# Holding back the modulation-weight loads while value tiles are turned through a DRAM scratch, in a one-core decoder layer

## The chip, the cores and the metric

The kernel runs on one core of a Trainium2 chip. The metric is the device time of one execution in microseconds. The kernel before was timed in three runs: 1776.6, 1780.31 and 1783.93 us, median 1780.31 us.

## What is computed

The reference is one layer of a decoder trunk, in float32, applied to a prompt of 256 tokens and to 8 single decode tokens (264 columns in all), with a model width of 2048. Cut to what matters here:

```
mod = silu(c) @ w_ada + b_ada                       # w_ada: 2048 x 12288, six 2048-wide rows of results
sh1, sc1, gt1, sh2, sc2, gt2 = split(mod, 6)
h = rmsnorm(x, g_pre_mix) * (1 + sc1) + sh1
z = h @ w_in                                        # inputs, gates and values of three token mixers
y_a = u * (W_s @ layernorm(v) + b)                  # mixer A: spatial gating
y_b = head_norm(gated recurrence, 8 heads) * silu   # mixer B (HGRN2)
y_c = head_norm(gated recurrence, 4 heads) * silu   # mixer C (GLA)
merged = sum_n sigmoid(z_gate[n]) * (y_n @ w_branch[n])
x  = x + gt1 * rmsnorm(merged @ w_out, g_post_mix)
h2 = rmsnorm(x, g_pre_mlp) * (1 + sc2) + sh2
x  = x + gt2 * rmsnorm(relu(h2 @ w_mlp_up)**2 @ w_mlp_down, g_post_mlp)
```

The six rows of `mod` are called rows 0 to 5. Rows 0 and 1 are needed at once; row 2 (gt1), 3 (sh2) and 4 (sc2) when the mixer half ends; row 5 (gt2) at the very end. The states of the recurrences are outputs too.

## The kernel before

**The stream.** Every large product takes its weights, 512 KB at a time, from `Stream` (L641): a load on SyncE's queue (L671) into one of four `raw` buffers, a rounded copy by ScalarE (`whi`, L679) and the rest by VectorE (`wlo`, L683), and then 24 matmuls into a PSUM tile `mm` (`granule`, L719). Such a step of 512 KB is called a granule. The counter `now` (L433) counts granules: `linear` (L813) runs granules one by one and calls `background()` (L791) after each, which adds one to `now` and does the side work that is due.

**The side work.** `background()` pumps three queues of generators: `bg` (the mixers' vector work), `bs` (the decode tokens' states) and `bt` (turning of tiles and tails). It calls `slot()` (L753) where small products have gathered: those of the mixers' levels, those of the decode states, and the modulation products. It ends with `rounds.tick()`.

**The modulation rounds.** `Rounds` (L371) computes rows 2, 3 and 4 of `mod` beside the mixers, 16 steps for each row. A step is 1 MB of `w_ada` in two loads of 512 KB on SyncE's queue (`load`, L379, the DMA on L388) and 16 recorded matmuls into `ada` (`steps`, L408). Steps are gathered into batches. The first of a batch goes into one of the two `araw` buffers, the others into blocks `b` of the general pool of 28 blocks. `tick` (L404) loads the next step when the batch is not full and `gap` (or `pace`) granules have gone by since the last load, `due` (L399) says that a full batch may be multiplied `land` granules after its last load. In the mixers `gap` is 2 and the batch is 1 where levels or decode states were pending in the last six granules, else 2; after branch 1, `pace` and the batch are 4. What is left when the output projection ends is loaded and multiplied at once by `rounds.drain()` (L1749). Row 5 has rounds of its own, six steps of which are loaded during the output projection (L1741).

**The value tiles.** Matmuls need some tiles with tokens on the partitions. `Rows` (L843) turns a block of 512 KB: VectorE transposes 32x32 squares (L856), `out` (L858) writes the block to the scratch `rows_d` in DRAM by one DMA of GpSimd's queue (L859), and `back` (L861) reads it with the squares in their new places by four DMAs of 128 KB on the same queue (L865). `come` (L881) waits at least `TURN_OUT` = 2 granules between the two, and whoever uses the tile waits `TURN_IN` = 2 granules after `back`. Eleven blocks are turned so while modulation rounds run: the values of both HGRN2 groups and of GLA, the decayed keys `kd` of each group, and the mixers' outputs.

**Order.** In the mixer and branch part (from L1182 to L1627) the order of instructions is written by hand on TensorE and GpSimd alone; on SyncE, ScalarE and VectorE the scheduler that builds the program places them, so a load can be issued ahead of one that was written before it. The same holds, with TensorE alone by hand, for the output projection (L1729 to L1754).

Of the kernel before, what the change touches and what calls it, by code (L numbers as in the profile page):

```python
# [57 lines left out]
LEVELS_HELD = 3  # L58
FETCHED = 3
AGE = 2  # L60
ADA_LAND = 4
FETCH = 256
FETCH_AT = 105
# [9 lines left out]
def hybrid_step_kernel(  # L73
# [11 lines left out]
    class Products:  # L85
# [4 lines left out]
        def matmul(self, out, w, x, **kw):  # L90
            self.n += 4 if w.dtype == F32 else 2
            return nc.tensor.matmul(out, w, x, **kw)  # L92
# [32 lines left out]
    def blk(shape=None, dt=F32):  # L125
        shape = shape or [P, 4, NT]
        return blkp.tile(shape, dt, tag="b", name=nm("b"))
# [118 lines left out]
    def rstd_small(ms, scale, out):  # L246

        n, w = out.shape
        xx, aa = tmp([P, 16], "sx")[0:n, 0:w], tmp([P, 16], "sa")[0:n, 0:w]
        c = 0  # L250
        for m in ms if isinstance(ms, list) else [ms]:
            V.tensor_scalar(xx[:, c:c + m.shape[1]], m, scale, EPS, ALU.mult, ALU.add)
            c += m.shape[1]
        V.tensor_scalar(out.bitcast(I32), xx.bitcast(I32), -0.5, 1597463007.0, ALU.mult, ALU.add)
        for _ in range(3):
            mul(aa, out, out)
            V.scalar_tensor_tensor(aa, aa, -0.5, xx, ALU.mult, ALU.mult)
            V.scalar_tensor_tensor(out, aa, 1.5, out, ALU.add, ALU.mult)
# [112 lines left out]
    class Rounds:  # L371
# [3 lines left out]
        def __init__(self):  # L375
            self.todo, self.ws, self.done, self.at = [], [], None, 0
            self.pace, self.batch, self.gap, self.land = 5, 1, 0, ADA_LAND

# [20 lines left out]
        def due(self):  # L399
            if self.ws:  # L400
                return self.full() and now[0] >= self.at + self.land
            return self.done is not None and not self.todo and now[0] >= self.at + 2 * ADA_LAND

        def tick(self):  # L404
            if self.todo and not self.full() and now[0] >= self.at + (self.gap or self.pace):
                self.load()

        def steps(self, n=None):  # L408
# [21 lines left out]

    rounds = Rounds()

    now = [0]  # L433

    class Queue:

# [316 lines left out]
    def slot():  # L753

        lv = [x for x in levels if x[0] + AGE <= now[0]][:2]
        sv = [x for x in samples if x[0] + AGE <= now[0]]
        late = max([now[0] - x[0] for x in lv] + [0]) >= AGE + SLOT_WAIT + 3
        while lv and not T.room(LEVEL_N * len(lv) + 16 * len(sv)) and (len(lv) == 2 or not late):
# [32 lines left out]
    def background():  # L791
# [10 lines left out]
        bs.pump(rate[1])  # L802
        wait = max([now[0] + 1 - AGE - x[0] for x in levels + samples] + [0])
        if not levels and samples and rounds.ws and rounds.full() and not rounds.due():
# [38 lines left out]
    class Rows:  # L843
# [13 lines left out]

        def out(self, i):  # L858
            nc.gpsimd.dma_start(rows_d[self.d0 + i], self.ts.pop(i))  # L859

        def back(self, i):  # L861

            t = blk([P, 1024])
            for q in range(4):
                nc.gpsimd.dma_start(  # L865
                    t[32 * q:32 * q + 32, :].rearrange("p (s c) -> p s c", s=4),
                    rows_d[self.d0 + i].rearrange("(s p) (q c) -> q p s c", s=4, q=4)[q],
                )
            self.rows.append(t.rearrange("p (s r k f) -> p r k s f", s=4, r=2, k=4))
            self.at = now[0]  # L870

        def gone(self):

            for i in range(len(self.blks)):
                for r in range(2):
                    self.half(i, r)
                    yield
                self.out(i)
            self.at = now[0]
# [676 lines left out]
    def branch(n, parts):  # L1556
        for m in range(8):
            if m == 0:
                yh, yl = parts()
            z = zin(9232 + n * D + m * CW)  # L1560
            gt = tmp([P, 2, NT], "gt")
            S.activation(gt, z, AF.Tanh, scale=0.5)
            pr = linear(w_branch[0, n], 0, 8, m * CW, CW, yh, yl)
            if n == 0 and m % 2 == 0:
                mg[m // 2] = blk()
            dst = pair(mg[m // 2], m % 2)

            if n == 0:
                V.scalar_tensor_tensor(dst, gt, 1.0, pr, ALU.add, ALU.mult)
            else:  # L1570
                V.scalar_tensor_tensor(gt, gt, 1.0, pr, ALU.add, ALU.mult)
                add(dst, dst, gt)
            if n == 2 and m % 2 == 1:
                a, b = blk(dt=F32R), blk(dt=F32R)
                split_tokens(mg[m // 2], a, b)
                mh.append(a)
                ml.append(b)
# [15 lines left out]
    def parts_b(gates):  # L1593
        for i in range(2):
            finish(i)
            o = Gs[i].o[0]
            V.scalar_tensor_tensor(o, o, hgnT, gates[i], ALU.mult, ALU.mult)
        return yparts([Gs[0].o[0], Gs[1].o[0]])
# [19 lines left out]
    narrow[1] = False  # L1618
    rounds.land = ADA_LAND + 1
    branch(1, lambda: parts_b(gates_b))  # L1620
# [461 lines left out]
```

## Time and profile before

| What | Value |
|---|---|
| median of three runs | 1780.31 us |
| the profiled execution | 1781.23 us |
| its span, first to last instruction | 1779.4 us |
| TensorE busy with matmuls | 1754.1 us (99%) |
| VectorE, ScalarE, GpSimd busy | 1197.1, 996.9, 184.7 us |
| mean granted TensorE clock | 0.998 |
| moved by DMA | 458.89 MB, mean 258 GB/s |
| loads of modulation weights by `Rounds` | 128, of 512 KB each |
| writes to the scratch, reads from it | 16 of 512 KB, 64 of 128 KB |

The span is what the profile's rows add up over; 1.8 us of the execution lie outside it. A row such as "PE mm L92" is a group of matmuls that go through the helper on line 92 and write a tile named `mm`; `ada` are the modulation products and `sm` the small products. SPq and POOLq are the instructions by which SyncE and GpSimd start a DMA. `x24` is a count. A number in brackets behind a row of the timeline is the time for which the engine had nothing to run before it, and behind the arrow stands what ended that.

### The profile page before, as it was taken

The page shows a single profiled execution, that of the slowest core. Times are in us where ns is not written, and L with a number is a line of the kernel's source. Part 1 is how long each engine was busy: PE and PEld are TensorE (multiplying, and loading weights), DVE is VectorE, ACT ScalarE, POOL GpSimd, SP SyncE. Part 2 cuts the span into 40 slices and gives each one's busy share as a digit, 9 for nine tenths or more (in the row PEclk, how much of TensorE's full clock was granted, in tenths as well). Part 3 has the DMA queues.
Part 4 walks back from the last instruction along what each step waited for, and adds up shares of the span by engine and source line. Part 5 has one row for each costly group of instructions (what it writes and reads, how often), then busy time and mean ns, then how long its engine had stood idle before and what let it go on. Part 6 is the DMA issues. An engine that isn't in the chain of part 4 may idle for free.

```text
span 1779.4 us, 43024 instructions
## 1 busy us (share of the span) xinstructions
PE 1754.1 (99%) x17334; PEld 1690.4 (95%) x17334; DVE 1197.1 (67%) x2105; ACT 996.9 (56%) x1808; POOL 184.7 (10%) x308
## 2 busy tenths in 40 slices
PE   7999999999999999999999999999999999999998
PEld 5899999999999999999999989999999999999997
DVE  5676779886787785566556666545666666666666
ACT  5444466776776666555445666545454545454544
POOL 4222011122121112210000010000000000000001
PEclk9999999999999999999999999999999999999999
DMA  9998877899998899998886847776666666666665
GB/s 349 400 349 296 281 245 237 285 314 315 317 305 266 301 326 304 332 356 275 281 281 215 310 125 235 238 260 201 192 200 192 199 192 198 194 197 195 196 196 167
DMA packets 335560, 458.89 MB, mean 258 GB/s; under 512 B 16226, under 2 KB 278224, under 8 KB 335360
## 3 DMA queue, kind: packets, MB, share of 16 engines
q1 hardware_dynamic: 312160, 381.05, 65.4%
q0 software_dynamic: 22560, 74.63, 12.2%
q8 instruction: 136, 2.23, 0.5%
q14 instruction: 64, 0.52, 0.1%
q10 hardware_dynamic: 640, 0.47, 0.1%
HBM read 435.99 MB, written 20.09 MB: 256 GB/s over the span
## 4 chain that ended last, share of the span: by engine, by line
PE 91%; DMA 4%; issue 3%; DVE 2%; ACT 1%; POOL 0%; SPq 0%; DVEq 0%; POOLq 0%; ACTq 0%
PE mm L92 82%; PE ada L92 5%; PE sm L92 4%; DMA raw<-in_w_in_dram 2%; DMA b<-in_w_ada_dram 1%; DMA rows_d<-b 1%; DVE wlo L683 1%; PE sm L96 1%; DMA b<-in_x_prompt_dram 0%; DVE b L142 0%; DMA b<-in_gla_w_up_dram 0%; DVE b L1821 0%; POOL b L865 0%; ACT whi L679 0%; DVE b L1358 0%
## 5 line engine op out<-in xcount | busy, mean ns | idle before, releaser
L92 PE MATMUL mm<-b,whi 128*128 128x264 f32 x9248 | 1577.9, 277 | 6.2 <-ACT whi L679 2.2
L92 PEld LDWEIGHTS mm<-b,whi 128*128 128x128 f32 x9248 | 1395.5, 189 | 26.3 <-issue 12.4
L92 PE MATMUL mm<-b,wlo 128*128 128x264 f32 x4624 | 1276.5, 276 | 0.2 <-DVE wlo L683 0.2
L683 DVE TENSOR_TENSOR wlo<-raw,whi 128x512 fp32r<-128x512 f32 x1118 | 756.6, 688 | 427.3 <-ACT whi L679 420.6
L679 ACT CAST whi<-raw 128x512 fp32r<-128x512 f32 x1118 | 679.6, 617 | 624.8 <-DVE wlo L683 312.1
L92 PEld LDWEIGHTS mm<-b,wlo 128*128 128x128 f32 x4624 | 874.2, 189 | 0.7 <-DVE wlo L683 0.4
L142 DVE TENSOR_TENSOR b<-b,mm 128x528 f32<-128x528 f32 (+1 forms) x137 | 95.4, 697 | 57.9 <-PE mm L92 51.7
L859 POOL DMA_DIRECT2D rows_d<-b x16 | 9.1, 566 | 776.8 <-DVE b L1698 685.3
L92 PE MATMUL ada<-b,cT 128*32 128x256 f32 (+1 forms) x1152 | 66.3, 367 | 2.4 <-DMA b<-in_w_ada_dram 2.1
L92 PEld LDWEIGHTS ada<-b,cT 128*32 128x32 f32 x1152 | 35.4, 112 | 25.1 <-DMA b<-in_w_ada_dram 5.6
L540 POOL DMA_DIRECT2D b<-in_w_ada_dram x64 | 46.3, 727 | 43.2 <-PE ada L92 32.6
L1319 POOL DMA_DIRECT2D out_dram<-st x32 | 23.5, 735 | 205.9 <-DVE st L1318 187.0
L865 POOL DMA_DIRECT2D b<-rows_d x64 | 35.2, 556 | 46.4 <-DMA rows_d<-b 20.5
L679 ACT CAST whi<-araw 128x512 fp32r<-128x512 f32 x38 | 23.2, 619 | 27.3 <-PE mm L92 23.4
L1318 DVE SCALAR_TENSOR_TENSOR st<-vbc,b,st 128x128 f32<-128x128 f32 (+1 forms) x96 | 32.3, 389 | 6.3 <-DMA vbc<-vs_d 4.4
L139 DVE TENSOR_TENSOR b<-b,b 128x512 f32<-128x512 f32 (+1 forms) x49 | 34.4, 717 | 2.3 <-ACT b L1385 1.0
L1316 ACT ACTIVATE st<-st,fs 128x128 f32<-128x128 f32 (+1 forms) x96 | 35.2, 426 | 0.0
L92 PE MATMUL ada<-araw,cT 128*32 128x256 f32 x512 | 34.8, 382 | 0.0
L683 DVE TENSOR_TENSOR wlo<-araw,whi 128x512 fp32r<-128x512 f32 x38 | 24.5, 685 | 1.3 <-ACT whi L679 1.3
L145 DVE TENSOR_TENSOR b<-b 128x1024 f32<-128x1024 f32 (+1 forms) x24 | 24.4, 1018 | 0.6 <-PE ada L92 0.4
L145 DVE TENSOR_TENSOR b<-gt,b 128x528 fp32r<-128x528 f32 x32 | 22.7, 708 | 3.1
L1895 ACT ACTIVATE b<-vt 128x528 fp32r<-128x528 f32 x32 | 22.8, 712 | 1.0
(312 smaller groups left out, 823.0 us busy)
## 6 DMA issues: line engine op xcount, KB each, us to landing
raw<-in_w_in_dram SPq DMA_DIRECT2D x225, 512.0 KB, 5.7
raw<-in_w_mlp_down_dram SPq DMA_DIRECT2D x128, 512.0 KB, 3.5
raw<-in_w_mlp_up_dram SPq DMA_DIRECT2D x125, 512.0 KB, 3.7
araw<-in_w_ada_dram SPq DMA_DIRECT2D x64, 512.0 KB, 6.8
b<-in_w_ada_dram SPq DMA_DIRECT2D x64, 512.0 KB, 7.0
b<-in_w_ada_dram POOLq DMA_DIRECT2D x48, 512.0 KB, 9.8
raw<-in_w_branch_dram SPq DMA_DIRECT2D x48, 512.0 KB, 5.5
raw<-in_w_out_dram SPq DMA_DIRECT2D x32, 512.0 KB, 4.9
```

The costliest lines, as they stand in the source:

```text
L92: return nc.tensor.matmul(out, w, x, **kw)
L139: V.tensor_tensor(o, a, b, op=ALU.mult)
L142: V.tensor_tensor(o, a, b, op=ALU.add)
L145: V.tensor_tensor(o, a, b, op=ALU.subtract)
L540: queue.dma_start(w[:, i], w1[k * P:(k + 1) * P, :, self.k0 * P:(self.k0 + self.n) * P])
L679: self.last = [S.copy(hi, raw).ins, None]
L683: self.last[1] = V.tensor_tensor(lo, raw, hi.bitcast(F32), op=ALU.subtract).ins
L865: nc.gpsimd.dma_start(t[32 * q:32 * q + 32, :].rearrange("p (s c) -> p s c", s=4), rows_d[self.d0 + i].rearrange("(s p) (q c) -> q p s c", ...
L1316: S.activation(st[:, i, :], st[:, i, :], AF.Copy, scale=fs[:, h0 + i, b:b + 1])
L1318: V.scalar_tensor_tensor(st[:, i, :], v[:, i, :], k[:, h0 + i, NP + b:NP + b + 1], st[:, i, :], ALU.mult, ALU.add)
L1319: nc.gpsimd.dma_start(G.s_out(b, h0, nh), st)
L1895: S.activation(apart(a), by_two(rl), AF.Square)
```

## The change

A second counter, `passes`, holds the granule up to which modulation weights are not asked for. Writing a block out sets it to three granules from now, reading one back sets it to two from now, and `tick` loads nothing before that granule. Nothing else is changed: `due`, `steps`, `drain` and `load` stay, and the loads of row 5 that are made by `pre.load` do not go through `tick`.

```
+PASS_OUT, PASS_IN = 3, 2
...
         def tick(self):
-            if self.todo and not self.full() and now[0] >= self.at + (self.gap or self.pace):
+            if self.todo and not self.full() and now[0] >= max(self.at + (self.gap or self.pace), passes[0]):
                 self.load()
...
-    now = [0]
+    now, passes = [0], [0]
...
         def out(self, i):
             nc.gpsimd.dma_start(rows_d[self.d0 + i], self.ts.pop(i))
+            passes[0] = now[0] + PASS_OUT
...
         def back(self, i):
...
             self.rows.append(t.rearrange("p (s r k f) -> p r k s f", s=4, r=2, k=4))
             self.at = now[0]
+            passes[0] = now[0] + PASS_IN
```

More of the change, by code (lines that the diff above doesn't have):

```diff
@@ L60 @@
 AGE = 2
+PASS_OUT, PASS_IN = 3, 2
 ADA_LAND = 4
@@ L404, in tick @@
         def tick(self):
-            if self.todo and not self.full() and now[0] >= self.at + (self.gap or self.pace):
+            if self.todo and not self.full() and now[0] >= max(self.at + (self.gap or self.pace), passes[0]):
                 self.load()
@@ L431, in hybrid_step_kernel @@
     rounds = Rounds()
-    now = [0]
+    now, passes = [0], [0]
     class Queue:
@@ L859, in out @@
             nc.gpsimd.dma_start(rows_d[self.d0 + i], self.ts.pop(i))
+            passes[0] = now[0] + PASS_OUT
         def back(self, i):
@@ L870, in back @@
             self.at = now[0]
+            passes[0] = now[0] + PASS_IN
         def gone(self):
```

## The prediction

> **What bounds the kernel now.** I read the page first, then TensorE's waits while the modulation rounds run (280 to 930 us), then the chain and the two queues around the one large wait.
>
> ```profile
> PE 1754.1 (99%) x17334; PEld 1690.4 (95%) x17334; DVE 1197.1 (67%) x2105; ACT 996.9 (56%) x1808; POOL 184.7 (10%) x308
> ```
>
> TensorE is busy for 1754.1 of a span of 1779.4 us, and the change removes no matmul. It can only gain where TensorE stands still, or runs slowly, because a load came late. Between 280 and 930 us TensorE's waits are these:
>
> ```profile
> PE mm L92 <- ACT whi L679: 2.2, 1, 2.2
> PE mm L92 <- ACT gt L1562: 0.9, 1, 0.9
> PE mm L92 <- ACT b L1253: 0.8, 1, 0.8
> PE mm L92 <- DVE wlo L683: 0.2, 1, 0.2
> ```
>
> Four waits, 4.1 us in all: that is nearly the whole prize. The wait for `L1253`, 0.8, is for ScalarE's eviction and not for a load; I leave it. The other three I follow to their place. In the timeline of TensorE they are:
>
> ```profile
> 598.22 0.49 PE L92 MATMUL mm<-b,whi 128*128 128x264 f32 x2 [2.20 <-ACT whi L679]
> 598.94 0.38 PE L92 MATMUL mm<-b,wlo 128*128 128x264 f32 x1 [0.23 <-DVE wlo L683]
> ...
> 766.67 0.49 PE L92 MATMUL mm<-b,whi 128*128 128x264 f32 x2 [0.90 <-ACT gt L1562]
> ```
>
> The first two are one stall. The windows and the chain show what follows it (the column after the four engines' and GpSimd's busy times is the granted clock, then the DMA engines' share and GB/s):
>
> ```profile
> 596.00:598.00 2.00, 0.01 (x1) 0.00 (x0) 0.00 (x0) 0.45 (x1) 0.00 (x0) 1.00 1.04 372
> 598.00:600.00 2.00, 1.55 (x8) 1.35 (x9) 1.80 (x3) 2.00 (x6) 0.00 (x0) 0.85 0.79 279
> 600.00:602.00 2.00, 2.00 (x11) 2.00 (x11) 2.00 (x5) 0.88 (x2) 0.00 (x0) 0.50 0.20 47
> ```
> ```profile
> 581.25 16.20 DMA raw<-in_w_in_dram
> ...
> 598.94 4.41 PE mm L92 x22
> ...
> 605.58 10.80 PE mm L92 x96
> ...
> 617.08 2.90 PE mm L92 x24
> ```
>
> At full clock 96 matmuls take 10.80 us, so a granule of 24 takes 2.70 and 22 take 2.48; behind the stall 22 took 4.41, at a granted clock of 0.50. So the stall costs 2.20 + 0.23 + 1.93 = 4.36 us. It ends when a stream load lands that was 16.20 us under way, where the usual is 5.7:
>
> ```profile
> raw<-in_w_in_dram SPq DMA_DIRECT2D x225, 512.0 KB, 5.7
> ...
> araw<-in_w_ada_dram SPq DMA_DIRECT2D x64, 512.0 KB, 6.8
> ```
>
> What lay before that load, on SyncE's queue and on GpSimd's, and how full the DMA engines were:
>
> ```profile
> 574.56 0.94 SPq L388 DMA_DIRECT2D araw<-in_w_ada_dram  x2
> 576.39 1.58 SPq L671 DMA_DIRECT2D raw<-in_w_in_dram  x2
> 578.01 2.45 SPq L388 DMA_DIRECT2D b<-in_w_ada_dram  x2
> 581.25 19.77 SPq L671 DMA_DIRECT2D raw<-in_w_in_dram  x5
> ```
> ```profile
> 575.49 0.56 POOL L859 DMA_DIRECT2D rows_d<-b  x1 [17.75 <-DVE b L856]
> ...
> 584.53 2.19 POOL L865 DMA_DIRECT2D b<-rows_d  x4 [4.69 <-DMA rows_d<-b]
> ```
> ```profile
> 580.00:585.00 5.00, 5.00 (x47) 5.00 (x46) 1.96 (x3) 4.87 (x6) 0.47 (x1) 1.00 1.03 379
> ```
>
> Two modulation steps (four loads, 2 MB) were asked for within 5 us, in the very granules in which a tile went out at 575.49 and came back at 584.53, and the DMA engines were full (share 1.03, 379 GB/s). This is the collision that the change is about.
>
> **The change part by part.** I count granules through the code. The tile that goes out at 575.49 does so in granule 110 and comes back in 113; the four loads above are asked for in 109 and 111. An earlier tile goes out in 102 and comes back in 105. Around here the modulation loads now come every four granules (a batch of one, `land` 4), then two granules apart in a batch of two.
>
> *The hold itself.* The first load that is held is that of granule 41; it goes in 42. Out in 60, 62, 66 and 70 and back in 65, 68, 69 and 75 then shut the loads off nearly without a break: what was loaded in 61, 66 and 68 now goes at about 73 and 77. That makes the rounds 8 granules late. Out 102 and back 105 hold the next load to 107; out 110 and back 113 hold the one after it to 115. So in 108 to 114 no step is asked for, where there were two, and the whole 2 MB (5.5 us at 379 GB/s) is gone from in front of the load of 581.25. Landing at 597.45 becomes about 592; the copy and the rest take 0.62 and 0.69 us,
>
> ```profile
> L683 DVE TENSOR_TENSOR wlo<-raw,whi 128x512 fp32r<-128x512 f32 x1118 | 756.6, 688 | 427.3 <-ACT whi L679 420.6
> L679 ACT CAST whi<-raw 128x512 fp32r<-128x512 f32 x1118 | 679.6, 617 | 624.8 <-DVE wlo L683 312.1
> ```
>
> and TensorE needs them at 596. The wait is gone with some 2.5 us to spare, and the half clock with it: -4.36 us. The bounds are 0 (the stall merely moves) and -4.36.
>
> [...]
>
> *The stall at 765.* Here the chain also leads to a stream load, and SyncE's queue is full of modulation loads:
>
> ```profile
> 753.90 10.98 DMA raw<-in_w_in_dram
> ```
> ```profile
> 752.90 0.90 SPq L388 DMA_DIRECT2D araw<-in_w_ada_dram  x2
> 753.90 0.46 SPq L671 DMA_DIRECT2D raw<-in_w_in_dram  x1
> 754.40 1.55 SPq L388 DMA_DIRECT2D b<-in_w_ada_dram  x1
> ...
> 759.01 4.60 SPq L388 DMA_DIRECT2D b<-in_w_ada_dram  x1
> ```
>
> These are the steps of granules 160 and 167. Tiles go out in 151 and 152 and come back in 156 and 158, so the change has loads at 155, 160, 167 and 171, where 153, 155, 160, 162 and 167 stood: one step less in the stretch. I take -0.90 (bounds 0 and -0.90).
>
> *What it adds: lateness.* No instruction is added, and nothing waits on a queue for the hold; SyncE simply gets these DMAs later, and the stream loads that were behind them go first. The 48 steps are shifted. By my count row 3 ends at 181 instead of 153, and row 4 has its last load at 244 and its last products at 249, instead of 214 and 219. The last two batches of row 4 before, of four steps and of two, and the first products behind the output projection are these:
>
> ```profile
> 895.24 3.59 PE ada L92 x64
> ...
> 923.32 1.86 PE ada L92 x32
> ...
> 1044.56 1.86 PE ada L92 x32
> ```
>
> The rows are wanted when the output projection has ended, in granule 262 (1044 us). So 13 granules are left, and lateness costs nothing on the path; the same `ada` matmuls run, in other gaps between granules. What they may cost is contention there: eight late loads now meet the twelve of row 5. In that stretch
>
> ```profile
> 970.00:1000.00 30.00, 30.00 (x269) 30.00 (x268) 19.50 (x43) 18.25 (x41) 0.00 (x0) 1.00 0.96 343
> ```
>
> TensorE is covered throughout at a DMA share of 0.96, and the pool of 28 blocks (16 hold operands and results there) lets no more than 12 into it at once, so the late blocks displace row 5's rather than add to them. Products that met in one `slot` may also part: a break in the stream costs about 0.2 us (the 24 matmuls of 617.08, behind small products, took 2.90). I take +1.0 for both, bounds -1 and +3.
>
> *What is late next.* With the stall gone TensorE gets to branch 1's first product of granule 122 sooner, at 612.6 instead of 617.0. Its operand comes from the tile that was turned here, by VectorE:
>
> ```profile
> 611.17 1.25 DVE L145 TENSOR_TENSOR b<-b,b 128x1056 fp32r<-128x1056 f32 x1
> ...
> 612.95 1.25 DVE L145 TENSOR_TENSOR b<-b,b 128x1056 fp32r<-128x1056 f32 x1
> ```
>
> It ends at 612.4. The cover of 4.6 us is gone but for 0.2, and the block behind it, wanted a granule later, ends at 614.2. The tile should also come back faster without 2 MB beside it. I take +1.0, bounds 0 and +4.
>
> *The sum.* -4.36 - 0.90 + 1.0 + 1.0 = -3.3 us. The profiled execution took 1781.23 us (span 1779.4 and 1.8 outside), which is 0.9 above the median of the runs; it becomes 1778.0, and the median 1780.31 becomes **1777.0 us**. That is 0.2% less. Within 0.5% (8.9 us) a measurement of this kernel, whose three runs before span 1776.6 to 1783.9, can hardly tell a change from none.
>
> **The rivals.**
>
> *The stall moves.* ScalarE, VectorE and SyncE are ordered by the scheduler here, and every shift of a load reorders them; loads held back come out together with the decode states' reads or with the next pass. The pass itself, 1 MB there and back, stays, and may do for a stall alone. For it: the share is near 1 in most of this stretch. Against it: in 280 to 930 us only two of TensorE's waits led back to a load. One new stall of the same size takes back 4.36: 1781.3. [...]
>
> *It does not do what it says.* The written order does not bind SyncE. The first step is written in granule 21 and multiplied in 33, twelve granules or some 33 us later; in the trace its load goes out 139 us ahead of the first products:
>
> ```profile
> 178.39 0.94 SPq L388 DMA_DIRECT2D araw<-in_w_ada_dram  x2
> ```
> ```profile
> L92 PE MATMUL ada<-araw,cT x512: 378/379/403, 316.9 to 1221.1; 128*32 128x256 f32 x171
> ```
>
> If blocks are free, the second load of a batch can so slip into the pass again. Then one step of the two stays, half of the 4.36 is won, and it ends at 1779.
>
> *Slower: the rounds end in the drain.* If the lateness passes the 13 granules that I count as left, up to four steps are loaded and multiplied when nothing else runs on TensorE: a load of 6.8 us from issue to landing by the row above, three more steps at 1 MB each in 8.3 us at 379 GB/s, and three instructions of ScalarE and VectorE on the row, some 2 us at the 0.6 to 0.7 of the rows above. For one step that is some 9 us on the path and for four 17, less the 3.3 won: 1786 to 1794, say 1790. It decides where one more batch of 17 granules is needed.
>
> **How the numbers follow.** I give the forecast 0.50, the moved stall 0.27, the slipped order 0.13 and the drain 0.10. Faster by over 0.5% needs 8.9 us where the three waits with their clock hold 5.3, so only scatter could give it: 0.03. Slower by over 0.5% is half of the drain and a few unnamed reorderings: 0.09. The rest, 0.88, is within. The range: downward both stalls, no cost, and the run-to-run scatter of about 3.5 us, 1771.5; upward the moved stall with the cost of granule 122 and some of the drain, 1787.
>
> **What would show it.** In the profile after, SyncE's queue has no modulation load between the out that is now at 575.49 and about 5 us after its reads; the stream load there lands in under 11 us; TensorE's wait for `whi` and the 0.50 window are gone; the wait at 765 is smaller. TensorE's busy total stays within 3 us of 1754.1, less some 2 us of half clock. The last `ada` of row 4 lies near 1008 us instead of 923. I am wrong if a wait of 2 us or more on a stream load stands elsewhere between 280 and 1045 us, or if `ada` and `sm` waits gather behind 1044 us.

## The result, and the profile after

The changed kernel takes 1776.03 us in the median of 15 runs (1775.17 to 1777.23), the kernel before 1780.21 us in the median of 15 (1776.5 to 1784.83). The ratio is 0.998, with a 95% interval of 0.9973 to 0.9988: 3.6 us, or 0.2%, clear of no change and well inside the 0.5% band. In the profiled execution the span went from 1779.4 to 1773.9 us.

Line numbers move on by one to three in the changed kernel: L92 is L93, L388 is L389, L859 and L865 are L860 and L867. From the page, the busy times:

```profile
PE 1751.5 (99%) x17334; PEld 1688.9 (95%) x17334; DVE 1197.1 (67%) x2107; ACT 997.3 (56%) x1808; POOL 184.7 (10%) x308
```

The same 17334 matmuls, 2.6 us less busy: 1.93 of that is the stretch at half clock, which is gone. TensorE's waits from 280 to 930 us, where four stood before:

```profile
PE mm L93 <- ACT b L1256: 0.8, 1, 0.8
PE mm L93 <- ACT gt L1565: 0.3, 1, 0.3
```

Only the wait that the prediction left alone is there (0.8), and a small new one near 465 us (0.3). The chain, the windows and the two queues around the old stall:

```profile
567.67 11.00 PE mm L93 x96
578.67 1.78 PE sm L93 x16
580.45 16.20 PE mm L93 x144
```
```profile
575.00:580.00 5.00, 5.00 (x47) 5.00 (x46) 3.17 (x5) 2.01 (x4) 0.16 (x1) 1.00 1.04 390
580.00:585.00 5.00, 5.00 (x47) 5.00 (x46) 1.97 (x3) 4.72 (x9) 2.58 (x5) 1.00 0.97 351
...
596.00:602.00 6.00, 6.00 (x56) 6.00 (x55) 6.00 (x10) 3.65 (x7) 0.00 (x0) 1.00 0.75 230
```
```profile
567.30 0.34 SPq L389 DMA_DIRECT2D araw<-in_w_ada_dram  x1
568.35 0.86 SPq L672 DMA_DIRECT2D raw<-in_w_in_dram  x1
569.30 0.46 SPq L389 DMA_DIRECT2D araw<-in_w_ada_dram  x1
569.80 0.42 SPq L389 DMA_DIRECT2D b<-in_w_ada_dram  x1
...
575.45 0.38 SPq L389 DMA_DIRECT2D b<-in_w_ada_dram  x1
```
```profile
574.60 0.56 POOL L860 DMA_DIRECT2D rows_d<-b  x1 [14.06 <-DVE b L857]
...
583.17 2.20 POOL L867 DMA_DIRECT2D b<-rows_d  x4
```

From 560 to 625 us the chain runs through matmuls alone, and TensorE is busy without a break (65.00 of 65.00 us) at a granted clock of 1.00. But the two queues do not show what the prediction said. Two modulation steps are still asked for near this tile; three of their four loads have moved 5 to 7 us ahead of the write at 574.60, where before two stood within a microsecond ahead of it and two behind it. What came of it is seen in the stream loads issued from 570 to 600 us, by the time from their issue to their landing. Before:

```profile
DMA to landing us min/median/max: 3.3/10.5/16.2
```

After:

```profile
DMA to landing us min/median/max: 4.6/5.7/6.6
```

Not all of the 5.5 us of span belongs to the change. Over the whole run, the kernel before has this row, whose longest wait (1.1 us) lies near 227 us, ahead of every load that the change touches; the row of the changed kernel follows:

```profile
PE mm L92 <- DVE b L142: 1.7, 4, 1.1
```
```profile
PE mm L93 <- DVE b L143: 0.7, 3, 0.3
```

The stalls near 597 and 765 us gave 4.36 and 0.90, and about 1 us is this wait, which comes and goes (below). That is 6.3 us, more than the 5.5: against it stand the new wait of 0.3 near 465 us and a wait in the first 60 us that no altered load comes near (for `in_g_post_mix`, 4.8 us before and 5.8 after). The medians, 4.2 us apart, are the better measure.

### The profile page after: what moved, and what is told of

Its sections match the earlier page's. It is cut to its first block, busy times and chain, and to the rows that moved or that the text cites. A ratio compares the mean times of both kernels' runs of the same rounds, so it can differ in the third digit from the quotient of the medians.

```text
span 1773.9 us, 43014 instructions
## 1 busy us (share of the span) xinstructions
PE 1751.5 (99%) x17334; PEld 1688.9 (95%) x17334; DVE 1197.1 (67%) x2107; ACT 997.3 (56%) x1808; POOL 184.7 (10%) x308
## 4 chain that ended last, share of the span: by engine, by line
PE 89%; issue 4%; DMA 3%; DVE 2%; POOL 1%; ACT 1%; SPq 0%; POOLq 0%; DVEq 0%; ACTq 0%
PE mm L93 81%; PE ada L93 5%; PE sm L93 3%; DMA rows_d<-b 1%; DMA b<-in_w_ada_dram 1%; POOL b L867 1%; PE sm L97 1%; DMA b<-in_x_prompt_dram 0%; DVE wlo L684 0%; DMA b<-rows_d 0%; DVE b L143 0%; DMA b<-in_gla_w_up_dram 0%; DVE b L1824 0%; DVE b L146 0%; DVE b L1361 0%
## 5 line engine op out<-in xcount | busy, mean ns | idle before, releaser
L93 PE MATMUL mm<-b,whi 128*128 128x264 f32 x9248 | 1576.5, 277 | 2.4 <-ACT b L1256 0.8
L93 PEld LDWEIGHTS mm<-b,whi 128*128 128x128 f32 x9248 | 1394.3, 189 | 21.9 <-issue 13.2
L93 PE MATMUL mm<-b,wlo 128*128 128x264 f32 x4624 | 1275.5, 276 | 0.0
L93 PEld LDWEIGHTS mm<-b,wlo 128*128 128x128 f32 x4624 | 873.5, 189 | 0.2
L860 POOL DMA_DIRECT2D rows_d<-b x16 | 9.1, 567 | 765.6 <-DVE b L1701 684.1
L93 PE MATMUL ada<-b,cT 128*32 128x256 f32 (+1 forms) x1184 | 66.9, 366 | 2.7 <-DMA b<-in_w_ada_dram 2.6
L93 PEld LDWEIGHTS ada<-b,cT 128*32 128x32 f32 x1184 | 36.6, 112 | 25.1 <-DMA b<-in_w_ada_dram 5.0
L867 POOL DMA_DIRECT2D b<-rows_d x64 | 35.3, 558 | 49.9 <-DMA rows_d<-b 21.2
L93 PE MATMUL ada<-araw,cT 128*32 128x256 f32 x480 | 32.5, 383 | 0.0
```

The source lines that it names most:

```text
L867: nc.gpsimd.dma_start(t[32 * q:32 * q + 32, :].rearrange("p (s c) -> p s c", s=4), rows_d[self.d0 + i].rearrange("(s p) (q c) -> q p s c", ...
```

## The experiments

All ratios are to runs of the kernel before that were timed together with the run, on the same chip. Medians of different groups can't be compared: the kernel before had 1780.21 us beside the changed kernel, 1779.15 (35 runs) beside e1 to e4, 1777.97 (29) beside e5 to e8 and 1777.86 (34) beside e9 to e12. "Largest landing" is the longest time from issue to landing of a stream load issued from 570 to 600 us, and "beside the out" is the number of modulation loads (512 KB each) that SyncE issued from 1.1 us ahead of the write to the scratch near 575 us to 8 us after it, both read from the traces. (With 2 us ahead of the write in place of 1.1 the count of e6 would be 1, and no other would change.) The last column has the waits from 560 to 620 and from 740 to 770 us. Every cell behind the medians is from one execution; since before and e1 are one program and differ by 2.3 us in the wait near 597, a single 0 there proves little, and the landings tell the groups apart better.

| Run | Ratio (95%) | Median us | Largest landing, us | Beside the out | TensorE's waits near 597 / 765 us |
|---|---|---|---|---|---|
| before | 1 | 1780.21 | 16.2 | 4 | 2.43 / 0.9 |
| e1, before again | 0.9997 (0.9988 to 1.0007) | 1778.22 | 13.5 | 4 | 0.12 / 1.6 |
| e9, a third step | 1.0024 (1.0015 to 1.0032) | 1781.18 | 14.6 | 5 | 0.72 / 2.8 in all |
| e10, one step held | 0.9991 (0.9982 to 0.9999) | 1776.04 | 10.1 | 2 | 0 / 0 |
| e3, one spot | 0.9983 (0.9974 to 0.9992) | 1776.61 | 8.7 | 2 | 0 / 0.8 |
| after | 0.998 (0.9973 to 0.9988) | 1776.03 | 6.6 | 1 | 0 / 0 |
| e2, hold from granule 90 | 0.9977 (0.9968 to 0.9986) | 1774.75 | 6.9 | 0 | 0 / 0 |
| e4, hold elsewhere | 0.9991 (0.998 to 1.0001) | 1776.94 | 6.6 | 0 | 0 / 0.2 |
| e5, out only | 0.9979 (0.997 to 0.9988) | 1774.53 | 7.0 | 0 | 0 / 0.2 |
| e6, in only | 1.0004 (0.9994 to 1.0013) | 1778.73 | 7.0 | 0 | 0 / 2.5 |
| e8, hold up to granule 89 | 0.9985 (0.9977 to 0.9994) | 1775.73 | 7.5 | 0 | 0 / 0 |
| e7, longer holds | 1.0057 (1.0044 to 1.007) | 1788.97 | 7.9 | 0 | 0 / 0.5 |
| e11, after again | 0.9991 (0.9981 to 1.0001) | 1775.27 | 7.4 | 1 | 0 / 0 |
| e12, e2 again | 0.9992 (0.9983 to 1.0001) | 1775.48 | 7.3 | 0 | 0 / 0 |

**The kernel before, once more.** No edit. The two traces of the same program tell how much of the stall is chance.

> The kernel before, unchanged, profiled once more. Collision theory (the stall near 596 us belongs to the placing of the loads): a wait of 1.5 to 2.5 us for the weight copy near 596 us and a stretch of half clock again, span within 3 us of 1779.4, ratio 1.000. Chance theory (the stall is a throw of the DMA engines that only some executions have, and the 15 runs of before lie 8 us apart because of it): no such wait, or another one elsewhere; span 1775 to 1783. The gap of 1.05 us near 227 us, ahead of every altered load, should be absent here by both if it is scatter.

The load is late again, on the same queue picture:

```profile
571.49 0.81 SPq L388 DMA_DIRECT2D araw<-in_w_ada_dram  x2
573.11 3.38 SPq L671 DMA_DIRECT2D raw<-in_w_in_dram  x2
576.53 1.52 SPq L388 DMA_DIRECT2D b<-in_w_ada_dram  x2
580.68 17.10 SPq L671 DMA_DIRECT2D raw<-in_w_in_dram  x5
```
```profile
580.68 13.52 DMA raw<-in_w_in_dram
```

It takes 2.7 us less than in the first trace, and TensorE waits 0.12 us where it waited 2.43, at a granted clock of 1.00; the span is 1775.5. So the late load is there in both executions, and the kernel stands at an edge here: landing times of 13.5 and 16.2 lie on the two sides of what the stream's lead covers at this place. Neither theory was right alone.

The lead is not the same everywhere. In the first trace of the kernel before, the loads from 725 to 745 us take nearly as long as the one that stalled, up to 15.0 us, and TensorE does not wait for them:

```profile
DMA to landing us min/median/max: 4.6/13.0/15.0
```

So what the stream had in hand covered 15.0 us there and did not cover 16.2 near 597 us. The wait near 227 us came again here with 0.8 us, so my expectation for it missed; in e3 and e4 it is 0.3.

**The hold from granule 90 on alone**, so that the mixers stay in place:

```
-... max(self.at + (self.gap or self.pace), passes[0]):
+... max(self.at + (self.gap or self.pace), passes[0] if now[0] >= 90 else 0):
```

> The hold acts from granule 90 on alone, so the mixers stay where they were (out in 102 and 110, back in 105 and 113) and the loads of 104, 109, 111 go to 107 and 115. Collision theory: no wait of TensorE on a stream load between 560 and 620 us, no half clock there, ratio 0.997 to 0.999. Reshuffle theory (the change gained because the early holds moved the mixers' passes two granules on, to 112 and 115, behind the loads of 109 and 111 that stayed): the stall remains, ratio 0.999 to 1.001.

Modulation loads go out at 554.82 and from 586.29 us, and none between:

```profile
554.82 0.82 SPq L389 DMA_DIRECT2D araw<-in_w_ada_dram  x2
559.40 26.82 SPq L672 DMA_DIRECT2D raw<-in_w_in_dram  x9
586.29 0.71 SPq L389 DMA_DIRECT2D b<-in_w_ada_dram  x1
```

No wait from 560 to 620 us, here or in e12, whose mean granted clock is 1.0; the ratio is 0.9977. At this pass this is the change as the prediction pictured it, and the collision theory holds: the mixers did not have to move.

**One spot.** No hold by passes; `tick` does nothing in granules 105 to 115.

```
-            if self.todo and not self.full() ...
+            if not 105 <= now[0] < 116 and self.todo and not self.full() ...
```

> No hold by passes; no modulation load is asked for in granules 105 to 115 alone, so loads stand at 104 and 116 and the pass at 110 and 113 has none beside it. Collision theory: the stall near 596 us and its half clock are gone, the 0.9 us near 765 us may stay, ratio 0.9975 to 0.999. Reshuffle theory: stall of about 2 us remains or comes again within 30 us, ratio 0.999 to 1.001.

The stall and the half clock are gone (no wait from 560 to 620 us, mean granted clock 1.0) and the ratio is 0.9983 (0.9974 to 0.9992): by the ratios this one place is worth most of the change. The queue shows that the order as written does not bind:

```profile
571.77 0.46 SPq L388 DMA_DIRECT2D araw<-in_w_ada_dram  x1
573.61 0.37 SPq L671 DMA_DIRECT2D raw<-in_w_in_dram  x1
574.09 1.33 SPq L388 DMA_DIRECT2D araw<-in_w_ada_dram  x1
575.52 17.16 SPq L671 DMA_DIRECT2D raw<-in_w_in_dram  x6
```

The step that is written in granule 116 was put here by the scheduler, some 20 us ahead of its written place and beside the write at 572.7; SyncE's waits ahead of its two loads (1.3 and 0.5 us) both end with TensorE. With 1 MB there and not 2, the worst landing is 8.7 us, and that is covered.

**Elsewhere.** The same edit with granules 78 to 89, where no tile passes.

> No hold by passes; no load in granules 78 to 89, where no tile passes. The mixers slip by two granules as in the changed kernel (out in 104 and 112, back in 107 and 115) while loads stand at 108 and 110, two granules ahead of the out in 112. Reshuffle theory: as fast as the changed kernel, ratio 0.997 to 0.999, no stall near 596 us. Collision theory in its strict form (any two steps within a pass stall): a wait of 1 us or more for a stream load between 570 and 610 us, ratio 0.999 to 1.002.

The mixers slip by two granules as in the changed kernel, the loads (issued from 564.82 to 571.19 us) go out ahead of the write at 575.97, and the stall is gone without any hold at a pass. So by the profile the reshuffle theory is half true as well: it does not matter here whether the steps or the pass have moved. The ratio, 0.9991 with an interval that reaches 1.0001, does not tell whether it gains as much as the changed kernel.

**Out only and in only.** `PASS_OUT, PASS_IN = 3, 0` and `0, 2`.

> PASS_OUT 3, PASS_IN 0: loads may come out beside the reads. They stand at 107 and 110, the tile goes out in 112 and back in 115, the next load is in 120. Collision theory: no stall near 596 us, since the step of 110 is all but in when the tile goes out; ratio 0.998 to 0.999. The last load of row 4 lies in granule 225, so the output projection has none beside row 5's.

> PASS_OUT 0, PASS_IN 2: loads stand at 109 and 111, the tile goes out in 112 and back in 115, as in the changed kernel. Collision theory: as fast as the changed kernel within 0.1%, no stall near 596 us, ratio 0.9975 to 0.999. If holding for the way out is what counts, a stall of over 1 us stands at some out that has a step in its own granule (63, 102, 155), and the ratio is 0.999 to 1.001.

Out only gains all of it, 0.9979. In only gains nothing, 1.0004 (0.9994 to 1.0013). That misses the collision theory's number; it is the ratio that was expected if holding for the way out is what counts, but the stall does not stand where that expectation put it. Nothing is late near 596 us, and the stall comes near 767. SyncE's queue, TensorE's waits from 740 to 770 us, the windows and two pieces of the chain of this kernel:

```profile
752.97 0.44 SPq L389 DMA_DIRECT2D b<-in_w_ada_dram  x1
753.46 0.95 SPq L389 DMA_DIRECT2D araw<-in_w_ada_dram  x2
754.82 14.42 SPq L672 DMA_DIRECT2D raw<-in_w_in_dram  x5
```
```profile
PE mm L93 <- ACT whi L680: 2.0, 2, 1.7
PE mm L93 <- DVE wlo L684: 0.5, 2, 0.2
```
```profile
768.00:770.00 2.00, 2.00 (x13) 2.00 (x12) 2.00 (x5) 1.39 (x4) 0.06 (x1) 0.58 0.66 224
770.00:772.00 2.00, 2.00 (x11) 1.90 (x10) 2.00 (x5) 2.00 (x5) 0.65 (x1) 0.57 1.04 327
```
```profile
735.79 16.20 DMA raw<-in_w_branch_dram
...
754.82 11.37 DMA raw<-in_w_in_dram
```

Two late landings follow each other in the chain. The first load was issued at 735.79, among the reads of two blocks (issued from 733.42 to 744.76) and behind four modulation loads issued from 724.96 to 727.45; the stream loads from 730 to 740 us took up to 17.1 us and cost TensorE 0.5 us near 751. The second was issued at 754.82, behind four more modulation loads (from 749.52 on), when the last block was already back, and its landing ends the wait of 1.73. So only the first of the two lies in a pass.

This is the rival "the stall moves" as it stood in the prediction, half clock (0.58 and 0.57 over the two windows) and all; the changed kernel has that hold as well, and does not show it.

**Longer holds.** `PASS_OUT, PASS_IN = 6, 4`.

> PASS_OUT 6, PASS_IN 4: the rounds get so late that row 4's last steps are loaded in granules 261 and 264, that is in the drain behind the output projection. Drain theory: TensorE stands still for 8 to 17 us there (load, products, the row's three instructions), ratio 1.001 to 1.007. Cover theory (the loads go out ahead of their place and the norms' work hides the rest): 0 to 4 us there, ratio 0.998 to 1.000.

The drain costs, and the slower rival is real. TensorE's waits from 1035 to 1050 us, and the clock there:

```profile
PE ada L93 <- DMA b<-in_w_ada_dram: 4.6, 2, 3.2
PE ada L93 <- ACT gt L363: 0.7, 1, 0.7
```
```profile
1044.00:1048.00 4.00, 2.31 (x20) 0.79 (x24) 2.25 (x6) 1.12 (x4) 0.00 (x0) 0.53 0.50 141
1048.00:1052.00 4.00, 4.00 (x38) 2.28 (x34) 2.16 (x8) 1.40 (x4) 1.26 (x2) 0.62 0.16 37
```

There are 5.3 us of waits and then some 6.8 us at half clock (an estimate from the 0.53 and 0.62 of these windows, taken as a mix of 1.00 and 0.50); the ratio is 1.0057 (1.0044 to 1.007), 11 us slower than the kernel before. The ratio is what the drain theory expected. The standstill of 5.3 us lies between the two theories (8 to 17 and 0 to 4); with the 3.4 us that the half clock costs by this estimate it comes near the 9 us that the prediction gave a single step. The drain isn't all of the loss: the same trace has 4.3 us of other waits between 400 and 1020 us. By the prediction's count the constants 3 and 2 end 13 granules short of this.

**The hold up to granule 89 alone.** The condition of e2 turned around.

> The hold acts up to granule 89 alone: the mixers move as in the changed kernel (out in 104 and 112), and loads stand at 108 and 110, then 120. Collision theory: the pass of 112 to 115 has only the tail of one step beside it, no stall over 0.5 us near 596 us, ratio 0.998 to 0.9995; the stall near 765 us may be back, since 155 to 162 have no hold. Hold theory (the late holds carry the gain): ratio 0.9995 to 1.001.

The ratio is 0.9985 (0.9977 to 0.9994), with no stall at either place. The holds at the passes of granule 100 and after, which the prediction took for the cause, are not needed when the earlier ones have moved the mixers.

**A third step, and one step less.** In e9 a batch of three and a gap of one in granules 110 to 115; in e10 the edit of e3 with granules 110 to 115, so that the step of 109 stays and that of 111 waits.

```
-            return len(self.ws) >= self.batch or left == 0
+            return len(self.ws) >= (3 if 110 <= now[0] < 116 else self.batch) or left == 0
-            if self.todo and ... now[0] >= self.at + (self.gap or self.pace):
+            if self.todo and ... now[0] >= self.at + (1 if 110 <= now[0] < 116 else self.gap or self.pace):
```

> The kernel before with a third step (1 MB more) asked for in the pass of granules 110 to 113: loads at 109, 110 and 111. Collision theory: the stream load that landed 13.5 to 16.2 us after its issue lands 2 to 3 us later still (16 to 19 us), TensorE waits 2.5 to 5 us near 596 us and runs a window at half clock, ratio 1.0005 to 1.003. Chance theory: as before, ratio 0.999 to 1.001 with a wait of 0 to 2.2 us there.

> The kernel before with the step of granule 111 held to 116, that of 109 left: half of the 2 MB goes from the pass. Collision theory: the load lands 2 to 3 us earlier (10.5 to 13 us), no wait over 0.3 us and no half clock near 596 us, the stall near 765 us stays as it falls; ratio 0.998 to 0.9995. If both steps are needed to be gone, a wait of 0.5 us or more stays, ratio 0.9995 to 1.001.

e10 came out much as expected: with 1 MB beside the write the worst landing is 10.1 us (10.5 to 13 was expected) and nothing waits, near 765 us either, where I expected no change. Its ratio is that of the changed kernel timed beside it (0.9991, e11 below), so, within the intervals, one step moved away from this place does as well as all the holds. e9 was no clean dose: the scheduler put the added step's loads at 567.87 and 571.05 us, largely ahead of the write at 572.02, so the late load took 14.6 us and the wait there was 0.72, less than I expected. The kernel is slower by 0.24% all the same. The steps behind it shifted, and the stretch from 740 to 770 us now holds waits of 2.8 us; that these make up the rest isn't shown.

**After and e2 once more, side by side.**

> The changed kernel once more, beside the next one on the same chip: ratio 0.997 to 0.999, no wait on a stream load over 0.4 us, and its runs within 3 us of each other.

> The hold from granule 90 on alone, once more. If leaving the early holds out is worth something (row 4's last load in 233 instead of 244), it is 0.5 to 1.5 us faster than the changed kernel in the same call; if not, the two agree within 0.5 us.

The ratios are 0.9991 (0.9981 to 1.0001) and 0.9992 (0.9983 to 1.0001), the medians 1775.27 and 1775.48 us: the two kernels are the same within what can be measured, and no version tried beats the changed one clearly. The kernel before ran at 1777.86 in the median here, 2.4 us under the first series, so the gain is 2.6 us by medians, its interval just reaches no change, and the ratio lies just outside the 0.997 to 0.999 that I expected. One run of e11 took 1781.49, which misses the expectation of 3 us of scatter. The profiled execution of e11, which took 1774.92, has no wait on a stream load; of the one that took 1781.49 there is no profile.

## Why the prediction was right, point by point

- **The bound and the size of the prize.** Right. TensorE is the bound, and only its waits for late loads could go. 1777.0 was forecast, 1776.03 measured, 0.2% as forecast. That it fits so well is partly luck: -5.26 for the two stalls was the size in one execution of the kernel before, the +2.0 of costs did not show, and the two errors point opposite ways. The medians give 4.2 us in the first series and 2.6 in the second.
- **The stall near 597 us, -4.36.** At this place the runs show it: with 4 or 5 modulation loads beside the write the worst stream load takes 13.5 to 16.2 us, with 2 it takes 8.7 to 10.1, with 0 or 1 it takes 6.6 to 7.9 (table), and TensorE waits in the first group alone. The block on its way is the smaller part of it. With no modulation load beside the write the worst is 6.9 us (e2). Four modulation loads with no block on the move, though with transfers of decode states of 256 KB on GpSimd's queue (three issued from 627.98 to 629.47 us), can be seen in the changed kernel, where they are issued from 630.19 to 634.16 us; the stream loads from 630 to 640 us have

```profile
DMA to landing us min/median/max: 10.6/11.6/11.9
```

  and TensorE does not wait. So most of the delay came with the modulation loads ahead of a stream load in the queue (11.9 us against the 6.9 of e2), and the pass adds some 2 to 4 us (an estimate, 13.5 and 16.2 against 11.9); no run has the four loads at 597 us without the block. The size is that of one execution. In e1 the same program waited 0.12 us there, so what the change removes is a stall of 0.1 to 4.4 us in the two executions seen. The kernel before is spread over 8.3 us in its first 15 runs and the changed kernel over 2.1, which would fit; but in the later series the changed kernel is spread over 6.9 us in 12 runs (e11) and the kernel before over 6.5 in 34. So the runs don't show that the spread comes from this stall.
- **"So in 108 to 114 no step is asked for."** This step failed. I let the mixers stay where they were. The early holds moved the slots in which the mixers' small products run, and the tile of granule 110 went out in 112; the loads fell in 109 and 111, not in 107 and 115. One of the four still went out beside the pass, at 575.45, so the sign that the prediction asked for (no modulation load from the out to 5 us after the reads) did not appear. Three were clear of the pass all the same, from the other side, and e2 and e4 show that the stall goes either way. The number was right with a wrong course behind it.
- **The stall near 765 us, -0.90.** The wait is gone in the changed kernel, in both of its traces. But the reason given, tiles on the move in 151 to 158, isn't what stands there: in the kernel before the last reads were issued from 742.94 to 744.14 us and landed 6.4 to 6.5 us after their issue, and the load that this wait leads back to was issued later, at 753.90. Beside it were six modulation loads, issued from 747.77 to 759.01; the changed kernel has four between 737 and 751 us and none from there to 768. The same program waits 1.6 us there in e1, so the size depends on the execution. That a hold at a pass is what removed it isn't shown.
- **Lateness.** Counted right: the last load of row 4 falls in 244, its last products in 249, and they stand in the chain 9 us ahead of the 1008 us forecast. Of these, 3.6 us are the products themselves, which in the kernel before had run ahead of this point, and the other 5.5 are as much as the whole gain in span:

```profile
998.89 3.59 PE ada L93 x64
```

  The cover held: from 930 to 1045 us TensorE idles 0.03 us, at a DMA share of 0.85 where it was 0.74 over the same stretch.

```profile
930.00:1045.00 115.00, 114.97 (x1115) 108.86 (x1117) 72.33 (x158) 65.64 (x140) 3.45 (x8) 1.00 0.85 295
```

  I took +1.0 for contention and for products that part; no wait shows it.
- **Granule 122, +1.0.** Oversized. The chain has no wait between 560 and 625 us; the tile was read back 1.4 us sooner (583.17 against 584.53), as the bound of 0 allowed.
- **The rivals.** The moved stall and the drain did not come with these constants, but both exist: e6 is the one, e7 the other. The slipped order is real too: in e3 and e9 the scheduler put loads ahead of their written place.

## What to carry to other kernels

When a kernel is bound by one engine, list that engine's waits and follow each to its transfer before pricing a change to transfers; the sum of these waits, with the slow stretches behind them, is the ceiling. A late transfer is not yet a wait: 15.0 us cost nothing at one place and 16.2 cost 4.4 at another. Take the profile of the kernel before twice where its runs are spread: the stall at the edge of the prefetch's cover was 2.4 us in one execution here and 0.1 in the next. Before a slow transfer is put down to two streams that meet, look for a place where one of them runs alone. And where slots and generators share one counter, a held load moves everything that waits for the same slot, so count the others' places anew, and read the order from the queue and not from the code.

## What the runs showed of the hardware

In two executions TensorE's granted clock fell to about half behind waits of about 2 us. In e6 the waits of 1.73 and 0.23 us were followed by about 3.4 us at half clock (an estimate: 0.58 and 0.57 over the windows from 768 to 772, taken as a mix of 1.00 and 0.50). In the kernel before 2.20 and 0.23 us were followed by as much (0.85, 0.50 and 0.79 over the windows from 598 to 604). In e1 a wait of 1.6 us, in the first of these two windows, was followed by none:

```profile
760.00:764.00 4.00, 2.41 (x22) 2.21 (x21) 1.29 (x2) 1.65 (x3) 0.00 (x0) 1.00 1.06 387
764.00:768.00 4.00, 4.00 (x38) 4.00 (x37) 2.93 (x5) 2.29 (x4) 0.00 (x0) 1.00 1.04 373
```

Whether e1 was spared by its shorter wait or by the moment at which it fell isn't shown.
